# Block sums of a down projection: from GpSimd instructions to accumulating DMAs, and activation differences from GpSimd to VectorE

## The chip, the core and the metric

The kernel runs on one NeuronCore of a Trainium2 chip. Its engines are named as in the profile: PE is TensorE (PEld its weight loads), DVE is VectorE, ACT is ScalarE, POOL is GpSimd, SP is SyncE, which here only issues DMAs. The metric is the device time of one execution in microseconds.

## The reference

One encoder block on 512 tokens of width 1024, in float32. Three token mixers (a bidirectional mLSTM, a neighbourhood attention, a cross-attention into 256 memory tokens) are merged by gates, and a gated feed-forward network with 2816 hidden channels follows:

```python
def conv_glu_ffn(h, w_up, w_conv, b_conv, w_down):
    a, u = jnp.split(h @ w_up, 2, axis=-1)
    return (jax.nn.gelu(dwconv3(a, w_conv, b_conv)) * u) @ w_down
...
x = x + conv_glu_ffn(rms_norm(x, ffn_norm_g[l]), w_ffn_up[l], w_ffn_conv[l], b_ffn_conv[l], w_ffn_down[l])
return rms_norm(x, final_norm_g)
```

The change lies in the last matrix product, `(512 x 2816) @ w_down (2816 x 1024)`, here called the down projection.

## The kernel before

**Three matmuls for one.** A float32 product is made from values split in a high and a low part: `mm3` issues high x high, high x low and low x high (L296, L297, L298). A weight block is loaded raw by SP (L203), its high part is made on ACT (L259 in the down projection, L274 elsewhere), the low part is the difference from the raw block on DVE (L260, L275). The tiles `w` that hold both parts have four buffers, so a block can be split only when PE has finished the block four places earlier.

**The down projection.** Its 2816 rows are 22 slices of 128. The first 12 slices go in six pairs (`NSP = 6`) through seven products of sums and differences instead of eight plain ones, in the manner of Strassen: `FORMS` names, for form 1 to 7, which activation quarters are subtracted, which weight blocks are added (sign 1) or subtracted (sign -1), or that a block is used alone. The last 10 slices (`NOK`) are multiplied plainly. `DOWN` lists 62 weight blocks in the order in which PE takes them; here they are numbered 0 to 61. Form 2 has blocks 0 to 7, form 4 blocks 8 to 16, form 5 blocks 17 to 24, form 7 blocks 25 to 33, form 1 blocks 34 to 42, form 3 blocks 43 to 50, form 6 blocks 51 to 58. In each of them six blocks belong to the form ("s" blocks, 6 matmuls each), and two or three plain ones ("k" blocks, 12 matmuls each) stand between. Blocks 59 to 61 are held for the end.

**Sums.** A block of forms 3, 4, 6 and 7 (24 in all) and of form 1 (6) comes as two blocks of 128x512 side by side in one 512 KB load. `emit_sum` adds or subtracts them into the first one on POOL (L225, `u<-u`, 30 instructions). For forms 1, 2, 5, 6 and 7 it also makes the three activation differences of a form, each for two pairs (L225, `s<-u`, 15 instructions). ACT and DVE split the activations into `uf` (L246, L247), with three pairs of buffers. All 45 sums are made by `in_turn`, which keeps them on POOL in the order of the program, after the last product of the GELU part (L1260).

**Raw tiles.** Blocks 0 to 5 use the three `raw` buffers that the rest of the kernel uses. From block 6 on they lie in "units", 14 big tiles shared with the activations; one unit takes two blocks, wide or narrow. `weights(key)` is called before each block's matmuls; it emits the loads up to 5 blocks ahead (`RAW_AHEAD`, 3, for the earlier ones), the sums up to 3 ahead and the splits up to 2 ahead. A scheduler then sets the order on each engine; every engine and each DMA queue works strictly in that order.

**After a form,** DVE adds its two product tiles into the output tiles `C_` (L1293, where the residual comes in, and L1295). `left` multiplies half of an output row block with the final gain on POOL (L1309, four in all).

Of the kernel before, what the change touches and what calls it, by code (L numbers as in the profile page):

```python
# [14 lines left out]
ALU = mybir.AluOpType  # L15
AX = mybir.AxisListType

P = 128
# [4 lines left out]
M = 256  # L23
DFF = 2816
FT = DFF // P
NSP = 6
NOK = FT - 2 * NSP
HELD = 3
HC = D // 2
# [96 lines left out]
DOWN0 = BINDEX[DOWN[0]][0]  # L126
# [3 lines left out]
def hybrid_block(ctx, tc, xT, memT, wflat, vecs, gbias, nabias, out):  # L130
    nc = tc.nc
    V, A, G, PE, SY = nc.vector, nc.scalar, nc.gpsimd, nc.tensor, nc.sync
# [12 lines left out]
    def nm(s):  # L145
        uid[0] += 1
        return f"{s}_{uid[0]}"

    def unit(dt=F32):
        return up.tile([P, UNIT], dt, tag="unit", name=nm("u"))  # L150

    def scr(n=512):
        return sp.tile([P, 512], F32, tag="scr", name=nm("s"))[:, :n]
# [28 lines left out]

    raws, split = {}, {}
    RAW_AHEAD, SPLIT_AHEAD = 3, 1
    st = {"raw": 0, "sum": DOWN0, "split": 0}
    uraw = []

    def emit_raw(i):
        key, n = BLOCKS[i]
        _, off, _ = BINDEX[key]  # L190
        if i < DOWN0 + NSP:
            r = wp.tile([P, BW], F32, tag="raw", name=nm("wr"), bufs=3)
        else:
            if not uraw:
                u = unit()
                uraw.extend((u[:, :2 * HC], u[:, 2 * HC:4 * HC]))
            r = uraw.pop(0)
        src = wflat[off:off + P * n].rearrange("(p n) -> p n", p=P)
        raws[i] = r
        if i < 2:  # L200
            cuts = (0, P, n // 2, n) if i == 0 else (0, n // 2, n)
            return [(r[:, a:b], src[:, a:b]) for a, b in zip(cuts, cuts[1:])]
        SY.dma_start(r[:, :n], src)  # L203
# [15 lines left out]

    ur, uf = [], {}  # L220

    def in_turn(dst, a, b, op):

        with tc.issue_after(st["g"]):
            st["g"] = G.tensor_tensor(dst, a, b, op=op).ins  # L225

    def emit_sum(i):

        key, n = BLOCKS[i]
        if key[0] != "s":  # L230
            return
        a, a2, _, w2, sign = FORMS[key[1]]
        p = key[2]
        if w2:
            r = raws[i]
            in_turn(r[:, :HC], r[:, :HC], r[:, HC:2 * HC], ALU.add if sign > 0 else ALU.subtract)
        if p % 2 == 0:
            v = ur[p // 2][:, :4 * S].rearrange("p (q k s) -> p q k s", q=2, k=2)
            q2 = lambda t: t.rearrange("p (q s) -> p q s", q=2)
            src = v[:, :, a[1], a[0] * M:(a[0] + 1) * M]  # L240
            if a2:
                d = q2(scr())
                in_turn(d, src, v[:, :, a2[1], a2[0] * M:(a2[0] + 1) * M], ALU.subtract)
                src = d
            h, l = [tp.tile([P, S], F32R, tag="E", name=nm("uf"), bufs=EB) for _ in range(2)]
            A.activation(q2(h), src, AF.Copy)  # L246
            V.tensor_tensor(q2(l), src, q2(h).bitcast(F32), op=ALU.subtract)  # L247
            uf[key[1], p // 2] = h, l
# [31 lines left out]
    def weights(key):  # L280

        i, _, n = BINDEX[key]
        last = len(BLOCKS) - 1
        while st["raw"] <= min(i + (5 if st["raw"] >= DOWN0 + NSP else RAW_AHEAD), last):
            emit_raw(st["raw"])
            st["raw"] += 1
        while st["sum"] <= min(i + 3, last):
            emit_sum(st["sum"])
            st["sum"] += 1
        while st["split"] <= min(i + (2 if st["split"] >= DOWN0 else SPLIT_AHEAD), last):  # L290
            emit_split(st["split"])
            st["split"] += 1
        return split.pop(i)
# [35 lines left out]

    A.dma_start(vec[:, :8], vecs[:, :8])  # L330
    w0, w1 = emit_raw(0), emit_raw(1)
    st["raw"] = 2
    load_x(0)
# [112 lines left out]
    def proj(key, XHs, XLs, n=S, bank=None, at={}):  # L446
        ws = weights(key)
        ps = (bank or mmps)()
        for k in range(KT):
            mm3(ps[:, :n], ws[k][0], ws[k][1], XHs[k], XLs[k], k == 0, k == KT - 1)  # L450
            if k in at:
                at[k]()
        return ps
# [3 lines left out]
    for k in range(KT):  # L457
        if k % 2 == 0:
            ws = weights(("mlq", k // 2))
        while done < min(KT, k + 1 + (k > 2)):  # L460
            x_part(done)
            done += 1
        wh, wl = ws[k % 2]
        for f in range(4):
            fs = slice(f * P, (f + 1) * P)
            mm3(ps_q[f], wh[:, fs], wl[:, fs], XH[k], XL[k], k == 0, k == KT - 1)
# [91 lines left out]
    for c, n in enumerate(TMW):  # L558
        pss = [(mmps if c % 2 else atps)() for _ in range(NT)]
        g = 2 if n == 512 else 4  # L560
# [552 lines left out]
    for f in range(4):  # L1113
# [5 lines left out]
        g = so[0][:, f * S:(f + 1) * S]  # L1119
# [117 lines left out]
    for f in range(FT):  # L1237
# [30 lines left out]
        if 3 <= f < 11:  # L1268
            t, g = (f - 3) % NT, (f - 3) // NT
            turns[t, g] = turn_out(x2v[g][:, :, t * P:(t + 1) * P])  # L1270
        if 6 <= f < 14:
            t, g = (f - 6) % NT, (f - 6) // NT
# [66 lines left out]
    last = NT - 1  # L1339
    for n, key in enumerate(DOWN):  # L1340
        wh, wl = weights(key)
        if key[0] == "s":
            _, i, p = key
            if p == 0 and i < 6:
                pm = [atps() for _ in range(2)]
            dst = pm if i < 6 else px[:2] if i == 7 else px[2:]
# [12 lines left out]
        _, g, j = key  # L1359
# [138 lines left out]
```

## Time and profile before

| | |
|---|---|
| median of 3 runs | 883.09 us (881.12 to 883.58) |
| the profiled execution | 882.28 us, span 880.1 us, mean granted TensorE clock 0.994 |
| down projection, first to last matmul | 735.86 to 871.2 us |
| from the last matmul to the end of the span | 9 us |
| POOL, `u<-u` sums of weight blocks (L225) | 30 instructions, 47.8 us |
| POOL, `s<-u` differences of activations (L225) | 15 instructions, 24.1 us |
| DVE, low parts of the down projection's blocks from units (L260) | 53 instructions, 56.6 us |

A view by stretches gives, for each stretch of the span, its length and how long each engine was busy in it, with the number of instructions in brackets, the granted clock, the DMA engines' busy share and GB/s. Matmuls overlap, so PE's busy time says only where it stood still; the distance from one matmul's start to the next says more. In a timeline a row is: start, duration, engine, line, operation, output and inputs, and in brackets the idle time before it with the instruction that ended it.

### The profile page before, as it was taken

To read this page: it belongs to the slowest core of one execution; us is meant where nothing else is said; L and a number is where in the kernel's file an instruction comes from. 1 tells how busy PE (TensorE), PEld (TensorE's weight loads), DVE (VectorE), ACT (ScalarE), POOL (GpSimd) and SP (SyncE) were. 2 spreads that over 40 slices of the span, in tenths; PEclk is the share of its full clock that TensorE was granted. 3 is DMA by queue.
4 is the path that set the end of the run, shared out by engine and by line. 5 is a ranking of instruction groups with operands and counts; after the bars stand their busy time and mean duration, and the time that the engine had idled before them with its cause. 6 is when DMAs were issued, how large, how long until landed. Compare 5 with 4: busy or idle time off the path is not lost.

```text
span 880.1 us, 12286 instructions
## 1 busy us (share of the span) xinstructions
PE 854.3 (97%) x4044; PEld 712.1 (81%) x4044; DVE 636.9 (72%) x1214; ACT 463.5 (53%) x975; POOL 211.1 (24%) x264
## 2 busy tenths in 40 slices
PE   9999999999999999999999999999999998898985
PEld 7898889988888888888888888888888886676755
DVE  6699677865477768987585477766666667886993
ACT  7465556765455668887444444344444444343442
POOL 1001100000105800760002112111111116465851
PEclk9999999999999999999999999999999999999999
DMA  8237654643346746987434324444322226356532
GB/s 266 91 106 227 205 159 148 199 131 100 128 132 201 189 144 213 253 234 219 150 110 136 107 96 141 147 146 145 117 96 96 96 72 238 96 191 207 212 132 96
DMA packets 73520, 135.75 MB, mean 154 GB/s; under 512 B 9832, under 2 KB 35048, under 8 KB 73456
## 3 DMA queue, kind: packets, MB, share of 16 engines
q1 hardware_dynamic: 65808, 128.51, 45.0%
q0 software_dynamic: 7360, 6.32, 3.4%
q8 instruction: 32, 0.52, 0.3%
q14 instruction: 32, 0.26, 0.1%
q10 hardware_dynamic: 288, 0.14, 0.1%
HBM read 120.23 MB, written 14.70 MB: 153 GB/s over the span
## 4 chain that ended last, share of the span: by engine, by line
PE 84%; DVE 5%; issue 3%; DMA 3%; POOL 2%; ACT 2%; SPq 0%; POOLq 0%; DVEq 0%; ACTq 0%
PE mm L297 25%; PE mm L298 24%; PE mm L296 24%; DVE w L260 2%; DMA u<-wflat 2%; PE at L297 2%; PE at L298 2%; PE at L296 2%; PE at L944 1%; POOL s L225 1%; DVE uf L247 1%; PE at L777 1%; DMA wr<-wflat 1%; PE at L779 1%; PE at L761 1%
## 5 line engine op out<-in xcount | busy, mean ns | idle before, releaser
L296 PE MATMUL mm<-u,w 128*128 128x512 f32 (+1 forms) x912 | 353.8, 388 | 0.4 <-ACT w L274 0.4
L297 PE MATMUL mm<-u,w 128*128 128x512 f32 (+1 forms) x912 | 352.2, 386 | 0.0
L298 PE MATMUL mm<-u,w 128*128 128x512 f32 (+1 forms) x912 | 352.1, 386 | 0.0
L274 ACT ACTIVATE w<-wr 128x512 fp32r<-128x512 f32 (+1 forms) x256 | 159.6, 627 | 146.2 <-PE mm L298 109.1
L275 DVE TENSOR_TENSOR w<-wr,w 128x512 fp32r<-128x512 f32 (+2 forms) x257 | 175.1, 686 | 71.5 <-ACT w L274 69.0
L298 PEld LDWEIGHTS mm<-u,w 128*128 128x128 f32 x912 | 171.4, 188 | 35.0 <-DVE w L275 0.7
L296 PEld LDWEIGHTS mm<-u,w 128*128 128x128 f32 x912 | 171.5, 188 | 34.5 <-ACT w L274 1.1
L297 PEld LDWEIGHTS mm<-u,w 128*128 128x128 f32 x912 | 171.5, 188 | 33.7 <-DVE u L303 0.5
L590 POOL DMA_DIRECT2D u<-nav_d x128 | 62.1, 501 | 102.0 <-PE at L944 51.5
L1260 POOL TENSOR_TENSOR s<-s,rb 128x512 f32<-128x512 f32 x22 | 37.4, 1699 | 188.7 <-DVE s L1259 181.0
L260 DVE TENSOR_TENSOR w<-u,w 128x512 fp32r<-128x512 f32 x53 | 56.6, 1100 | 6.9 <-ACT w L259 6.9
L225 POOL TENSOR_TENSOR u<-u 128x512 f32<-128x512 f32 x30 | 47.8, 1612 | 31.6 <-DVE w L260 20.3
L259 ACT ACTIVATE w<-u 128x512 fp32r<-128x512 f32 x53 | 32.4, 624 | 35.5 <-PE mm L298 23.2
L297 PE MATMUL mm<-w,u 128*128 128x512 f32 x116 | 46.0, 397 | 4.6 <-DVE w L260 4.5
L296 PE MATMUL mm<-w,u 128*128 128x512 f32 x116 | 45.6, 394 | 0.0
L298 PE MATMUL mm<-w,u 128*128 128x512 f32 x116 | 45.2, 390 | 0.0
L297 PEld LDWEIGHTS mm<-w,u 128*128 128x128 f32 x116 | 21.9, 189 | 11.5 <-DVE w L260 7.2
L1228 POOL TENSOR_TENSOR acc<-acc,s 128x512 f32<-128x512 f32 x7 | 9.0, 1288 | 91.6 <-ACT s L1227 91.6
L483 ACT ACTIVATE s<-pad,vec 128x512 f32<-128x512 f32 x30 | 24.4, 813 | 6.2 <-DVE pad L481 5.3
L246 ACT ACTIVATE uf<-s 128x512 fp32r<-128x512 f32 x15 | 9.4, 629 | 32.4 <-POOL s L225 31.3
L296 PE MATMUL at<-w,uf 128*128 128x512 f32 x60 | 24.2, 403 | 2.3 <-ACT uf L246 2.3
L296 PEld LDWEIGHTS mm<-w,u 128*128 128x128 f32 x116 | 21.9, 189 | 4.7
(300 smaller groups left out, 1238.0 us busy)
## 6 DMA issues: line engine op xcount, KB each, us to landing
wr<-wflat SPq DMA_DIRECT2D x124, 512.0 KB, 3.4
u<-wflat SPq DMA_DIRECT2D x30, 512.0 KB, 4.4
td<-s SPq DMA_DIRECT2D x160, 64.0 KB, 2.0
U<-td SPq DMA_DIRECT2D x40, 256.0 KB, 3.6
u<-wflat SPq DMA_DIRECT2D x26, 256.0 KB, 3.3
s<-xT SPq DMA_DIRECT2D x24, 256.0 KB, 4.2
nab<-nabias SPq DMA_DIRECT2D x16, 256.0 KB, 4.0
u<-nav_d POOLq DMA_DIRECT2D x128, 32.0 KB, 3.7
```

Of the source, the lines that this page charges most:

```text
L225: st["g"] = G.tensor_tensor(dst, a, b, op=op).ins
L246: A.activation(q2(h), src, AF.Copy)
L259: A.activation(h, r[:, :HC], AF.Copy)
L260: V.tensor_tensor(l, r[:, :HC], h.bitcast(F32), op=ALU.subtract)
L274: A.activation(h[:, u:v], src, AF.Copy)
L275: V.tensor_tensor(l[:, u:v], src, h[:, u:v].bitcast(F32), op=ALU.subtract)
L296: PE.matmul(ps, lh, rh, start=start, stop=False)
L297: PE.matmul(ps, lh, rl, start=False, stop=False)
L298: st["mm"] = PE.matmul(ps, ll, rh, start=False, stop=stop).ins
L483: A.activation(t1, pad[:, 0:512], AF.Identity, scale=vcol(w, i), bias=vcol(b, i))
L590: G.dma_start(vw[r * 32:(r + 1) * 32, i * 256:(i + 1) * 256], nav_v[hf, r, CW[b]:CW[b] + 32, hp * 256:(hp + 1) * 256])
L1260: st["g"] = G.tensor_tensor(c, c, rb2, op=ALU.mult).ins
```

## The change

The 24 sums of weight blocks with sign 1 are no longer made by an instruction. SP loads only the first block (256 KB) of the two; the second one is fetched from HBM by a DMA of POOL's queue that adds into the first block's tile (`accum_op`, L236 of the changed kernel). It can be issued only when the first block has landed. The 6 subtractions of form 1 and the 15 differences of activations become DVE instructions (L247 and L254 there). A unit now takes four blocks (two for form 1), loads run up to 9 blocks ahead, the accumulating DMAs are emitted up to 5 ahead, and subtractions and differences up to 3 ahead. `in_turn` is gone; POOL keeps the accumulating DMAs in order among themselves and after the last L1260 (now L1274).

```diff
-    st = {"raw": 0, "sum": DOWN0, "split": 0}
+    st = {"raw": 0, "sum": DOWN0, "form": DOWN0, "split": 0}
...
+        src = wflat[off:off + P * n].rearrange("(p n) -> p n", p=P)
         if i < DOWN0 + NSP:
             r = wp.tile([P, BW], F32, tag="raw", name=nm("wr"), bufs=3)
         else:
+            both = key[:2] == ("s", 1)
+            if both and len(uraw) % 2:
+                uraw.pop(0)
             if not uraw:
                 u = unit()
-                uraw.extend((u[:, :2 * HC], u[:, 2 * HC:4 * HC]))
-            r = uraw.pop(0)
-        src = wflat[off:off + P * n].rearrange("(p n) -> p n", p=P)
+                uraw.extend((u, j * HC) for j in range(4))
+            u, a = uraw.pop(0)
+            if both:
+                uraw.pop(0)
+            r = raws[i] = u[:, a:a + HC * (2 if both else 1)]
+            if n > HC and not both:
+                st[i] = src
+                src = src[:, :HC]
+                n = HC
...
-    def in_turn(dst, a, b, op):
-
-        with tc.issue_after(st["g"]):
-            st["g"] = G.tensor_tensor(dst, a, b, op=op).ins
-
     def emit_sum(i):
+
+        if i in st:
+            with tc.issue_after(st["g"]):
+                st["g"] = G.dma_start(raws[i], st.pop(i)[:, HC:], accum_op=ALU.add).ins
+
+    def emit_form(i):
...
-        if w2:
+        if sign < 0:
             r = raws[i]
-            in_turn(r[:, :HC], r[:, :HC], r[:, HC:2 * HC], ALU.add if sign > 0 else ALU.subtract)
+            V.tensor_tensor(r[:, :HC], r[:, :HC], r[:, HC:2 * HC], op=ALU.subtract)
...
             if a2:
                 d = q2(scr())
-                in_turn(d, src, v[:, :, a2[1], a2[0] * M:(a2[0] + 1) * M], ALU.subtract)
+                V.tensor_tensor(d, src, v[:, :, a2[1], a2[0] * M:(a2[0] + 1) * M], op=ALU.subtract)
                 src = d
...
-        while st["raw"] <= min(i + (5 if st["raw"] >= DOWN0 + NSP else RAW_AHEAD), last):
+        while st["raw"] <= min(i + (9 if st["raw"] >= DOWN0 + NSP else RAW_AHEAD), last):
             emit_raw(st["raw"])
             st["raw"] += 1
-        while st["sum"] <= min(i + 3, last):
+        while st["sum"] <= min(i + 5, st["raw"] - 1):
             emit_sum(st["sum"])
             st["sum"] += 1
+        while st["form"] <= min(i + 3, last):
+            emit_form(st["form"])
+            st["form"] += 1
```

PE's order is unchanged, and so is every engine's up to about the last step of the feed-forward's up projection. Three places show how the rest moves.

POOL's queue from the last GELU product on, before (`s_...<-u_...` is a difference of activations, `u_...<-u_...` a sum of weight blocks):

```order
L1260 TENSOR_TENSOR s_7196<-s_7196,rb_5543 128x512
L225 TENSOR_TENSOR s_7208<-u_5382 128x512
L225 TENSOR_TENSOR s_7266<-u_5383 128x512
L225 TENSOR_TENSOR u_7295<-u_7295 128x512 x2
L225 TENSOR_TENSOR u_7316<-u_7316 128x512
L225 TENSOR_TENSOR u_7357<-u_7357 128x512
L225 TENSOR_TENSOR u_7391<-u_7391 128x512 x2
L225 TENSOR_TENSOR s_7464<-u_5381 128x512
```

The same place in the changed kernel (L1274 is the GELU product, L1323 the product with the final gain):

```order
L1274 TENSOR_TENSOR s_7196<-s_7196,rb_5543 128x512
L236 DMA u_7283<-wflat 128x512 x2
L236 DMA u_7288<-wflat 128x512 x2
L236 DMA u_7322<-wflat 128x512 x2
L236 DMA u_7448<-wflat 128x512
L236 DMA u_7517<-wflat 128x512 x3
L236 DMA u_7573<-wflat 128x512 x2
L236 DMA u_7751<-wflat 128x512
L1323 TENSOR_TENSOR u_7246<-u_7246,gf_7247 128x512
```

Where POOL computed 45 sums it now issues 24 DMAs; the first two are for blocks 8 and 9, which lie in `u_7283`.

DVE where form 2 ends and form 4 begins, before (L260 low part of a block, L247 of activations, L1293 the additions after form 2; `w_7344`, `w_7359` and `w_7380` are blocks 8, 9 and 10):

```order
L260 TENSOR_TENSOR w_7323<-u_7283,w_7323 128x512
L260 TENSOR_TENSOR w_7344<-u_7295,w_7344 128x512
L260 TENSOR_TENSOR w_7359<-u_7295,w_7359 128x512
L1293 TENSOR_TENSOR u_7246<-U_6173,at_7256 128x512
L1293 TENSOR_TENSOR u_7246<-U_6260,at_7257 128x512
L1293 TENSOR_TENSOR u_7246<-U_6509,at_7256 128x512
L1293 TENSOR_TENSOR u_7246<-U_6591,at_7257 128x512
L260 TENSOR_TENSOR w_7380<-u_7316,w_7380 128x512
```

And in the changed kernel (L271 low part of a block, L258 of activations, L254 a difference of activations, L1307 the additions; `w_7349` and `w_7364` are blocks 8 and 9):

```order
L271 TENSOR_TENSOR w_7328<-u_7283,w_7328 128x512
L258 TENSOR_TENSOR uf_7381<-u_5382,uf_7380 128x512
L271 TENSOR_TENSOR w_7349<-u_7283,w_7349 128x512
L254 TENSOR_TENSOR s_7466<-u_5381 128x512
L254 TENSOR_TENSOR s_7496<-u_5382 128x512
L254 TENSOR_TENSOR s_7541<-u_5383 128x512
L254 TENSOR_TENSOR s_7586<-u_5381 128x512
L1307 TENSOR_TENSOR u_7246<-U_6173,at_7256 128x512
L1307 TENSOR_TENSOR u_7246<-U_6260,at_7257 128x512
L1307 TENSOR_TENSOR u_7246<-U_6509,at_7256 128x512
L1307 TENSOR_TENSOR u_7246<-U_6591,at_7257 128x512
L271 TENSOR_TENSOR w_7364<-u_7283,w_7364 128x512
```

Block 9's low part, which stood ahead of the four additions, now stands behind them, and four differences for the later forms 5 and 1 stand there too; block 8's waits for the first accumulating DMA.

DVE a little earlier, in the last GELU step, in the changed kernel (L1271 and L1273 belong to the GELU, L1280 takes POOL's product, `w_7272` and `w_7291` are blocks 3 and 4):

```order
L1271 SCALAR_TENSOR_TENSOR s_7200<-s_7200,s_7196 128x512
L258 TENSOR_TENSOR uf_7211<-s_7208,uf_7210 128x512
L254 TENSOR_TENSOR s_7266<-u_5383 128x512
L1273 SCALAR_TENSOR_TENSOR s_7196<-s_7200,s_7196 128x512
L271 TENSOR_TENSOR w_7272<-wr_7251,w_7272 128x512
L258 TENSOR_TENSOR uf_7269<-s_7266,uf_7268 128x512
L1280 TENSOR_TENSOR s_7196<-mm_7217,s_7196 128x512
L271 TENSOR_TENSOR w_7291<-wr_7264,w_7291 128x512
```

The differences of form 2 (`s_7208`, two rows above the first one shown, and `s_7266`) and a low part of activations have come in ahead of L1273, which POOL's last GELU product waits for.

## The prediction

> **What bounds the kernel now.** First the page: the engines' shares and the slices.
>
> ```profile
> PE 854.3 (97%) x4044; PEld 712.1 (81%) x4044; DVE 636.9 (72%) x1214; ACT 463.5 (53%) x975; POOL 211.1 (24%) x264
> PE   9999999999999999999999999999999998898985
> POOL 1001100000105800760002112111111116465851
> ```
>
> PE is the bound everywhere but in the last seven slices, where POOL becomes busy. Those slices are the down projection, so I cut it into stretches at PE's longer gaps. Columns: length, then busy us (and instructions) of PE, PEld, DVE, ACT, POOL, granted clock, DMA share, GB/s.
>
> ```profile
> 735.85:871.20 135.35, 120.03 (x502) 93.56 (x500) 106.61 (x120) 53.00 (x96) 79.33 (x51) 0.97 0.47 161
> ...
> 735.85:749.40 13.55, 10.59 (x38) 7.92 (x37) 11.53 (x11) 7.03 (x12) 11.92 (x8) 0.87 0.57 211
> 749.40:761.00 11.60, 9.02 (x38) 6.50 (x36) 11.60 (x11) 3.98 (x7) 7.92 (x5) 1.00 0.31 90
> 761.00:789.30 28.30, 28.30 (x125) 23.40 (x126) 21.52 (x29) 11.05 (x19) 11.40 (x8) 1.00 0.57 186
> 789.30:806.00 16.70, 13.30 (x53) 9.45 (x52) 10.39 (x12) 5.24 (x10) 9.52 (x7) 0.96 0.40 132
> 806.00:820.00 14.00, 14.00 (x58) 11.31 (x57) 11.26 (x16) 8.10 (x16) 11.12 (x7) 0.92 0.67 238
> 820.00:834.00 14.00, 11.88 (x51) 9.14 (x50) 14.00 (x17) 4.91 (x10) 11.61 (x9) 1.00 0.73 263
> 834.00:851.00 17.00, 12.74 (x50) 8.93 (x51) 16.70 (x14) 7.85 (x14) 14.72 (x9) 1.00 0.49 170
> 851.00:871.20 20.20, 20.20 (x98) 16.92 (x96) 9.62 (x18) 4.85 (x10) 1.12 (x2) 1.00 0.07 27
> ```
>
> What would these matmuls take without a gap? PE's timeline gives the pace: the first two rows are 11 starts apart, 2.49 us, so 0.2264 us each; after a gap (third row) come starts 0.42 us apart (the last two).
>
> ```profile
> 735.86 0.39 PE L296 MATMUL at<-w,uf 128*128 128x512 f32 x1
> ...
> 738.35 0.39 PE L298 MATMUL at<-w,uf 128*128 128x512 f32 x1
> 741.08 0.50 PE L296 MATMUL at<-w,uf 128*128 128x512 f32 x1 [2.34 <-ACT uf L246]
> ...
> 743.97 0.63 PE L297 MATMUL at<-w,uf 128*128 128x512 f32 x1
> 744.39 0.63 PE L298 MATMUL at<-w,uf 128*128 128x512 f32 x1
> ```
>
> The stretch runs 502 matmuls, one of them mostly before it, and 18 (6 on each of three lines, at the end) are half as wide: 483 x 0.2264 + 18 x 0.113 = 111.4 us, and the last one's own end 0.3, against 135.35. PE loses **23.6 us**. By stretch (length less count x 0.2264): 4.9, 3.0, 0, 4.7, 0.9, 2.5, 5.7, and 0 at the end; the rest is matmuls that a border counts twice. The long loss-free stretch 761 to 789 matters most. It contains the same kinds of blocks.
>
> Who ends these gaps, among PE's waits from 735.8 to 871.2 (total, times, longest):
>
> ```profile
> PE mm L297 <- DVE w L260: 10.5, 8, 3.0
> PE at L296 <- ACT uf L246: 2.3, 1, 2.3
> ```
>
> So the low part of a block comes late from DVE. DVE is busy for 97 of the 115 us up to 851: not the bound in sum, but in places. Its timeline and POOL's say why:
>
> ```profile
> 745.92 1.77 DVE L260 TENSOR_TENSOR w<-wr,w 128x512 fp32r<-128x512 f32 x1
> 752.72 5.15 DVE L260 TENSOR_TENSOR w<-u,w 128x512 fp32r<-128x512 f32 x3
> 757.80 2.46 DVE L1293 TENSOR_TENSOR u<-U,at 128x512 f32<-128x512 f32 x4
> 761.39 1.88 DVE L260 TENSOR_TENSOR w<-u,w 128x512 fp32r<-128x512 f32 x3
> ...
> 742.03 10.22 POOL L225 TENSOR_TENSOR u<-u 128x512 f32<-128x512 f32 x6
> 752.21 5.11 POOL L225 TENSOR_TENSOR s<-u 128x512 f32<-128x512 f32 x3
> 774.95 1.74 POOL L225 TENSOR_TENSOR u<-u 128x512 f32<-128x512 f32 x1 [17.63 <-DVE w L260]
> ```
>
> While POOL computes (742 to 757.3, at 1.70 us an instruction), DVE's low parts also go one per 1.7 us; when POOL stops, the same instruction takes 0.63 (three in 1.88). The two engines take turns. From 757.3 to 774.95 POOL rests, and there PE loses nothing after 761. This is the present bound of the stage: 45 sums on POOL, which are slow themselves and slow DVE.
>
> **The change part by part.** *Removed:* 45 POOL instructions, 47.8 + 24.1 us, and with them DVE's slow turns.
>
> ```profile
> L260 DVE TENSOR_TENSOR w<-u,w 128x512 fp32r<-128x512 f32 x53 | 56.6, 1100 | 6.9 <-ACT w L259 6.9
> L225 POOL TENSOR_TENSOR u<-u 128x512 f32<-128x512 f32 x30 | 47.8, 1612 | 31.6 <-DVE w L260 20.3 <-DMA u<-wflat 11.1
> L225 POOL TENSOR_TENSOR s<-u 128x512 f32<-128x512 f32 x15 | 24.1, 1615 | 0.0
> ```
>
> *Added on DVE:* 6 + 15 instructions of the same shape, at the undisturbed spacing of 0.61 to 0.63 us (757.80 and 761.39 above): 13 us. DVE then has about 104 instructions up to 851 (110 in the stretches above, less those counted twice) plus 20 of the new ones, 124 x 0.61 = 76 us, in the 91.5 us that PE needs for that part (115.15 - 23.6). That is 83%. In 761 to 789 DVE was 76% busy, partly against POOL, and PE lost nothing, so I expect few losses; the in-order places must be looked at singly.
>
> *Block 4.* DVE's L1280 waits for POOL's last GELU product, and block 4's low part stands behind it. Before:
>
> ```profile
> 731.50 0.69 DVE L481 TENSOR_TENSOR pad<-mm,rb 128x512 f32<-128x512 f32 x1
> 736.71 0.69 DVE L1259 SCALAR_TENSOR_TENSOR s<-s,s 128x512 f32<-128x512 f32 x1 [0.70 <-ACT s L1258]
> 737.48 1.66 POOL L1260 TENSOR_TENSOR s<-s,rb 128x512 f32<-128x512 f32 x1 [8.48 <-DVE s L1259]
> ```
>
> Three more DVE instructions now stand ahead of L1259 (L1273 of the changed kernel), 1.8 us, of which 0.7 fits into the wait shown: POOL's product ends at about 739.14 + 1.1 = 740.2, block 4's low part is there two DVE steps later, 741.5. PE reaches block 4 after four blocks of 6 x 0.227 = 1.36 us, at 741.3, and needs the low part 0.23 later: 0 to 0.7 us lost, I take 0.3. In return the 2.34 us wait of 741.08 goes: the differences of form 2 no longer queue behind that product.
>
> *Blocks 8 and 9.* The first two accumulating DMAs are issued at 740.2, one after the other. No accumulating DMA is in the trace. The nearest are POOL's plain 128x512 DMAs, first row their time on POOL, second from issue to landing, and SP's loads of two blocks and of one:
>
> ```profile
> L540 POOL DMA_DIRECT2D nav_d<-nv x8: 531/532/782, 85.6 to 98.1; - x8
> DMA to landing us min/median/max: 2.5/3.7/4.7
> ...
> u<-wflat SPq DMA_DIRECT2D x30, 512.0 KB, 4.4
> u<-wflat SPq DMA_DIRECT2D x26, 256.0 KB, 3.3
> ```
>
> Reading the destination as well makes it 512 KB of reads: bounds 2.5 us (nothing extra) and 4.7 + 4.4 = 9.1 us (a second pass after the first), I take 4.7, nearest the POOL rows. Block 8 lands at 745, its parts are made by 746.3 (ACT 0.63, DVE 0.69); PE wants it at 735.86 + 13.6 = 749.5. Then DVE does four differences and four additions, 8 x 0.61 = 4.9, and block 9's low part is ready at about 751.8; PE wants it at 749.5 + 1.36 + 0.23 = 751.1. Lost: 0.7, up to 5 with a 9.1 us landing; I take 1.2.
>
> *Later blocks.* A unit holds four blocks (two in form 1) and at least four units take turns, so the load of a first half can go out eight blocks or more (over 14 us) before its use: 3.3 for the load and even 9.1 for the accumulation are hidden. POOL's queue holds only these 24 DMAs (24 x 0.53 = 13 us) and four products of L1309. After each form, four additions (2.5 us) stand ahead of a low part that PE wants 4 to 5.4 us after the form's last product: covered. I allow 2.0 for what I have not seen (0 to 4.5).
>
> *DMA engines.* The share times length over the stretches up to 851 is 62 us of full use. A plain 256 KB takes 0.76 us of all 16 engines (161 GB/s at share 0.47). Taking 24 away leaves 44. POOL's own queue is slower per byte, 6.32 MB in 3.4% of the span, 1.24 us for 256 KB:
>
> ```profile
> q0 software_dynamic: 7360, 6.32, 3.4%
> ```
>
> So one accumulation costs between 0.76 and 2 x 1.24 = 2.5 us of all engines; I take 1.5 (one read more at the plain rate): 44 + 36 = 80 us of 95, hidden.
>
> *Half clock.* In 735.85 to 749.4 and 806 to 820 the granted clock is below 1; the timeline has 18 starts that lie 0.35 to 0.5 apart like those of 743.97, together 3.4 us of the 23.6. Gaps of 2 us should be gone: 0.5 left (0 to 3.4).
>
> Sum: 0.3 + 1.2 + 2.0 + 0.5 = 4.0 us left of 23.6, so **19.6 us gained**. 882.28 (the profiled execution; 0.8 under the median of 883.09) - 19.6 = 862.7, as a median 863.5. Everything ahead of 735 and the 9 us behind the last matmul stay.
>
> **The rivals.** *Late accumulations (R1).* The landing is 9 us instead of 4.7, blocks 8 and 9 cost 4 us more, and DVE, waiting in order at block 8, shifts what follows: 868 to 872. For it: an operation that no row shows. Against: the later ones are still early.
>
> *DMA engines decide (R2).* With price c per accumulation the stage needs 44 + 24c; beyond 95.5 us (c = 2.15) the engines set the end. At my upper bound of 2.5 that is 104, a time of 872; at c = 3.0 the gain is gone. *Slower (R3)* is the same resource beyond that point: at c = 3.4, some 4.5 times a plain copy, 125.6 us against 115.15, 893. For it: only the silence of the trace; against: 2.5 already counts every byte twice at the slow queue's rate.
>
> *The gaps stay (R4).* They come from in-order queues and splits only two blocks ahead, not from POOL, and the 13 us on DVE fill what POOL left: 874 to 883. For it: DVE at 83%. Against: 761 to 789.
>
> *POOL starves (R5).* If descriptors had to wait for DVE, each issue would wait for an instruction of 0.69 or for several. But while DVE did the same low parts (19 of them at 678 ns), POOL issued its 128 DMAs evenly:
>
> ```profile
> L275 DVE TENSOR_TENSOR w<-wr,w 128x512 fp32r<-128x512 f32 x19 | 12.8, 678 | 1.0 <-ACT w L274 0.9
> ...
> L590 POOL DMA_DIRECT2D u<-nav_d x128: 489/493/583, 273.8 to 398.7; - x128
> ```
>
> Three instructions' wait for each of the first two would cost 2 x 2.1 = 4.2 us at block 9: 868. The Trainium skill speaks against this change here: "SBUF — State Buffer", section "Summary: rules for kernel authors", tells authors who hide a GpSimd-issued DMA under a DVE operation to use the other queues, since descriptor generation starves while DVE is in a 2x or 4x mode. By that rule R5 would be likely; the trace does not agree for this instruction, 583 ns being the longest of the 128.
>
> **How the numbers follow.** Forecast 0.58 (860 to 868); R1 0.10; R2 0.11; R4 0.08; R5 0.03; R3 0.10. Time 863.5. The low end is every loss gone (23.6 off, 859.5), rounded to 860; the high end takes in R1, R5, R2 to past c = 2.5 and some of R4, 877; R3, the end of R2 and half of R4 are left out, 0.19. About 0.3% (2.6 us) is what a measurement can tell from no change. Faster: forecast, R1, R5, R2 but 0.01 and 0.04 of R4, 0.85; same 0.05; slower R3, 0.10.
>
> **What would show it.** Right: no L225-like work on POOL, 24 DMAs there of about half a us each; low parts (L271) at 0.6 to 0.7 us throughout; PE's loss from 735.9 to the last matmul 2 to 6 us, most of it before 753. Wrong: PE or ACT waiting for accumulated blocks beyond block 12 (R2, R3, with the DMA share near 1), DVE without a gap while PE waits (R4), POOL DMAs of over 1 us (R5). If accumulations take over 2.15 us of all engines each, the forecast falls.

## The result and the profile after

The changed kernel takes 871.26 us (median of 4 runs, 869.96 to 872.84) beside 883.34 us for the kernel before (881.12 to 884.72). The ratio is 0.9866, with a 95% interval from 0.984 to 0.9893. The change makes the kernel faster by 12.1 us, where 19.6 were predicted; the time lies inside the predicted range, 7.8 us above the predicted time.

The profiled execution took 871.15 us, its span is 869.4. The page of the changed kernel, the engines' shares and POOL's slices:

```profile
PE 851.0 (98%) x4044; PEld 713.2 (82%) x4044; DVE 619.4 (71%) x1235; ACT 464.1 (53%) x975; POOL 160.1 (18%) x243
...
POOL 2001100000104810742001202111111111221401
```

POOL's last seven slices, which read 6465851 before, now read 1221401. The down projection in stretches of the changed kernel (columns as before: length, then busy us and instructions of PE, PEld, DVE, ACT, POOL, granted clock, DMA share, GB/s; the last row is the whole of it):

```profile
735.07:748.60 13.53, 13.53 (x61) 11.22 (x60) 9.54 (x17) 6.89 (x13) 7.62 (x7) 1.00 1.07 326
748.60:761.00 12.40, 10.02 (x38) 7.77 (x37) 11.24 (x19) 4.70 (x8) 1.11 (x2) 0.86 0.83 191
761.00:789.30 28.30, 28.30 (x127) 23.43 (x126) 20.44 (x33) 13.25 (x22) 4.12 (x5) 1.00 0.71 188
...
802.00:819.00 17.00, 14.28 (x56) 11.30 (x55) 12.73 (x16) 6.98 (x13) 9.00 (x10) 0.90 0.92 233
819.00:834.00 15.00, 12.50 (x51) 9.15 (x51) 8.02 (x16) 6.71 (x15) 5.13 (x5) 1.00 1.01 227
...
735.07:840.00 104.93, 96.57 (x404) 77.38 (x403) 77.93 (x123) 47.15 (x84) 28.40 (x29) 0.97 0.78 205
735.07:860.50 125.43, 117.07 (x502) 94.58 (x500) 86.85 (x138) 52.60 (x95) 29.52 (x31) 0.97 0.67 176
```

In PE's timeline the first and the last start of a matmul lie 125.2 us apart. Less the 111.4 us that the matmuls need, PE loses **13.8 us**, where it lost 23.7 before: of the 12.1 us, 9.9 come from this stage in the two profiled executions. The stage also starts 0.8 us earlier (735.07 instead of 735.86); over all kernels below its start varies from 735.07 to 736.88, so a difference of a microsecond between two of them can arise ahead of it. The loss sits in three places, 748 to 761, 802 to 819 and 819 to 836; the stretches between lose nothing. Who ends PE's gaps (total, times, longest):

```profile
PE mm L311 <- DVE w L271: 3.5, 2, 2.7
PE at L311 <- DVE w L271: 2.9, 3, 2.4
PE at L310 <- ACT w L270: 2.0, 2, 1.7
```

**First place: block 9.** Here are POOL's and DVE's rows of the changed kernel, one fence each:

```profile
736.65 2.28 POOL L1274 TENSOR_TENSOR s<-s,rb 128x512 f32<-128x512 f32 x1 [9.61 <-DVE s L1273]
738.87 5.39 POOL L236 DMA_DIRECT2D u<-wflat  x6
```

```profile
746.66 0.69 DVE L271 TENSOR_TENSOR w<-u,w 128x512 fp32r<-128x512 f32 x1 [2.80 <-ACT w L270]
747.27 2.49 DVE L254 TENSOR_TENSOR s<-u 128x512 f32<-128x512 f32 x4
749.68 2.48 DVE L1307 TENSOR_TENSOR u<-U,at 128x512 f32<-128x512 f32 x4
752.07 1.89 DVE L271 TENSOR_TENSOR w<-u,w 128x512 fp32r<-128x512 f32 x3
```

POOL's last GELU product ends at 738.9, and six accumulating DMAs are issued behind it. The first one, issued at 738.87 for block 8, lands after 7.0 us, the second one, for block 9, after 8.3; the DMA engines' share is 1.07 in that stretch. DVE stands still for 2.80 us, until block 8 has landed and ACT has made its high part, takes block 8 at 746.66, then the eight instructions that stand ahead of block 9, whose low part is started at 752.07. PE stands still for 2.5 us, and for some microseconds behind it the granted clock is low (0.86 in that stretch).

**Second place: DVE beside POOL's products.** DVE and POOL around 801:

```profile
800.81 5.53 DVE L271 TENSOR_TENSOR w<-u,w 128x512 fp32r<-128x512 f32 x1
```

```profile
801.13 1.62 POOL L1323 TENSOR_TENSOR u<-u,gf 128x512 f32<-128x512 f32 x1
802.38 2.12 POOL L236 DMA_DIRECT2D u<-wflat  x2
803.52 2.26 POOL L1323 TENSOR_TENSOR u<-u,gf 128x512 f32<-128x512 f32 x1
```

One low part lasts 5.53 us instead of 0.69. It ends when the second of two products with the final gain does; between the products POOL issues two accumulating DMAs. PE stands still for 2.9 us.

**Third place: a held block.** ACT's instructions for blocks 59 and 60, which PE needs only at the end, and a row of the chain (the waits, followed back from the last instruction):

```profile
827.65 0.63 ACT L270 ACTIVATE u<-u 128x512 fp32r<-128x512 f32 x1 [6.59 <-DMA u<-wflat]
829.55 0.63 ACT L270 ACTIVATE u<-u 128x512 fp32r<-128x512 f32 x1 [0.75 <-DMA u<-wflat]
```

```profile
817.17 12.35 DMA u<-wflat
```

ACT waits 6.59 us for the plain load of block 59, which was issued at 816.67 and took 10.9 us while the DMA engines were full (share 1.01 from 819 to 834). The chain's row is the load of block 60, 12.35 us; block 61's took 13.9. Blocks 47 to 50 are queued behind the parts of these held blocks, on ACT or on DVE, and PE waits for blocks 47, 48 and 50 in five gaps of 1.87, 0.50, 0.42, 0.58 and 0.92 us, 4.3 us together.

What the new operations cost, from the groups, queues and DMA issues of the page, and from the view of L236 (duration in ns least/median/most; landing in us in the last row):

```profile
L271 DVE TENSOR_TENSOR w<-u,w 128x512 fp32r<-128x512 f32 x53 | 40.5, 779 | 23.5 <-ACT w L270 23.3
...
q0 software_dynamic: 10816, 12.61, 7.7%
...
u<-wflat SPq DMA_DIRECT2D x50, 256.0 KB, 5.4
u<-wflat POOLq DMA_DIRECT2D x24, 256.0 KB, 8.4
```

```profile
L236 POOL DMA_DIRECT2D u<-wflat x24: 853/902/2563, 738.9 to 824.1; - x24
...
DMA to landing us min/median/max: 4.1/8.4/13.2
```

The low parts went from 1100 to 779 ns. An accumulation takes POOL 0.9 us and lands after 8.4 us; the queue's share gives (7.7% x 869.4 - 3.4% x 880.1) / 24 = 1.54 us of all 16 DMA engines for each.

### The profile page after: what moved, and what is told of

It is laid out like the page before. It is cut to its first block, busy times and chain, and to the rows that moved or that the text cites. A ratio compares the mean times of both kernels' runs of the same rounds, so it can differ in the third digit from the quotient of the medians.

```text
span 869.4 us, 12253 instructions
## 1 busy us (share of the span) xinstructions
PE 851.0 (98%) x4044; PEld 713.2 (82%) x4044; DVE 619.4 (71%) x1235; ACT 464.1 (53%) x975; POOL 160.1 (18%) x243
## 3 DMA queue, kind: packets, MB, share of 16 engines
q0 software_dynamic: 10816, 12.61, 7.7%
## 4 chain that ended last, share of the span: by engine, by line
PE 89%; DMA 3%; issue 3%; DVE 3%; ACT 1%; POOL 1%; SPq 0%; POOLq 0%; DVEq 0%; ACTq 0%
PE mm L311 25%; PE mm L310 25%; PE mm L312 25%; DMA u<-wflat 3%; PE at L311 3%; PE at L312 2%; PE at L310 2%; DVE w L271 1%; PE at L958 1%; PE at L791 1%; PE at L793 1%; PE at L775 1%; POOL s L1274 0%; PE at L925 0%; PE at L924 0%
## 5 line engine op out<-in xcount | busy, mean ns | idle before, releaser
L1274 POOL TENSOR_TENSOR s<-s,rb 128x512 f32<-128x512 f32 x22 | 37.9, 1721 | 190.0 <-DVE s L1273 182.3
L271 DVE TENSOR_TENSOR w<-u,w 128x512 fp32r<-128x512 f32 x53 | 40.5, 779 | 23.5 <-ACT w L270 23.3
L236 POOL DMA_DIRECT2D u<-wflat x24 | 21.4, 1175 | 62.4 <-DVE u L1309 27.3
L311 PEld LDWEIGHTS mm<-w,u 128*128 128x128 f32 x116 | 22.2, 192 | 8.9 <-DVE w L271 4.3
L312 PEld LDWEIGHTS mm<-w,u 128*128 128x128 f32 x116 | 22.2, 191 | 4.7
L310 PEld LDWEIGHTS mm<-w,u 128*128 128x128 f32 x116 | 22.2, 192 | 4.6
```

The source lines that it names most:

```text
L236: st["g"] = G.dma_start(raws[i], st.pop(i)[:, HC:], accum_op=ALU.add).ins
L271: V.tensor_tensor(l, r[:, :HC], h.bitcast(F32), op=ALU.subtract)
L310: PE.matmul(ps, lh, rh, start=start, stop=False)
L311: PE.matmul(ps, lh, rl, start=False, stop=False)
L312: st["mm"] = PE.matmul(ps, ll, rh, start=False, stop=stop).ins
L1274: st["g"] = G.tensor_tensor(c, c, rb2, op=ALU.mult).ins
```

## The experiments

PE's loss is worked out as above for each kernel: the distance from the first to the last start in the down projection less 111.4 us.

| kernel | median us (lowest to highest) | ratio to before (95%) | PE's loss |
|---|---|---|---|
| changed kernel | 871.26 (869.96 to 872.84) | 0.9866 (0.984 to 0.9893) | 13.8 |
| 1 differences alone on DVE | 873.55 (872.01 to 874.24) | 0.9891 (0.9872 to 0.991) | 15.2 |
| 2 accumulating DMAs alone | 880.65 (879.43 to 881.54) | 0.9971 (0.9961 to 0.998) | 22.5 |
| 3 all sums on DVE | 860.78 (860.13 to 861.94) | 0.9752 (0.9731 to 0.9773) | 2.5 |
| 4 plain DMAs | 862.56 (861.8 to 864.03) | 0.9771 (0.9754 to 0.9787) | 4.8 |
| 5 no second blocks | 858.71 (858.15 to 859.12) | 0.9723 (0.9709 to 0.9738) | 0.1 |
| 6 final gain on DVE | 871.8 (871.36 to 873.73) | 0.9876 (0.9861 to 0.9891) | 13.9 |
| 7 held blocks' parts late | 863.12 (861.65 to 865.08) | 0.9775 (0.9754 to 0.9795) | 6.1 |
| 8 as 7, accumulations early | 862.52 (861.61 to 863.6) | 0.9756 (0.9736 to 0.9776) | 3.8 |
| 9 as 8, final gain on DVE | 861.25 (860.56 to 862.45) | 0.9744 (0.9727 to 0.9761) | 3.2 |
| 10 as 3, final gain on DVE | 858.42 (858.29 to 858.72) | 0.9711 (0.9697 to 0.9726) | 0.3 |
| 11 as 9, only two of them early | 860.39 (859.8 to 861.34) | 0.9742 (0.9726 to 0.9759) | 1.4 |

The kernel before beside them had medians from 883.02 to 883.96.

### 1 and 2: the two parts of the change, each alone

Experiment 1 is the kernel before with the differences moved:

```diff
-                in_turn(d, src, v[:, :, a2[1], a2[0] * M:(a2[0] + 1) * M], ALU.subtract)
+                V.tensor_tensor(d, src, v[:, :, a2[1], a2[0] * M:(a2[0] + 1) * M], op=ALU.subtract)
```

> The kernel before with one part of the change: the 15 differences of activations on VectorE, the 30 sums of weight blocks still on GpSimd. If GpSimd's computing instructions cost the time (themselves and by slowing VectorE), a third of them is gone (24 of 72 us) and the wait of 2.3 us near block 2 too: PE's loss in the down projection falls from 23.6 to about 16, 875 us (871 to 879). If only the accumulating DMAs bring the gain, nothing changes: 882 to 884.

Experiment 2 is the changed kernel with the differences back on POOL:

```diff
-                V.tensor_tensor(d, src, v[:, :, a2[1], a2[0] * M:(a2[0] + 1) * M], op=ALU.subtract)
+                with tc.issue_after(st["g"]):
+                    st["g"] = G.tensor_tensor(d, src, v[:, :, a2[1], a2[0] * M:(a2[0] + 1) * M], op=ALU.subtract).ins
```

> The changed kernel with the 15 differences of activations left on GpSimd, in one order with the accumulating DMAs. By the same theory 24 us of GpSimd computing come back, each of these instructions slows one or two of VectorE to 1.7 us and stands ahead of DMAs: loss about 17 to 20 us instead of 13.8, 875 us (872 to 879). If the differences are indifferent: 871.

Measured: 873.55 and 880.65. PE's waits in experiment 1, all for low parts (the 2.34 us wait for ACT is gone):

```profile
PE at L297 <- DVE w L260: 8.2, 6, 3.4
PE mm L297 <- DVE w L260: 2.4, 2, 1.7
```

The 15 differences alone bring 9.8 us, the accumulating DMAs alone 2.7, outside what was expected (some 8, at least 4); together 12.5, about the 12.1 of the whole change. In experiment 2 the first rows are PE's longest waits, then one row of DVE and two of POOL:

```profile
PE at L311 <- ACT w L271: 7.9, 1, 7.9
PE at L311 <- ACT uf L258: 2.3, 1, 2.3
```

```profile
743.77 6.80 DVE L272 TENSOR_TENSOR w<-wr,w 128x512 fp32r<-128x512 f32 x1
```

```profile
742.04 5.44 POOL L236 DMA_DIRECT2D u<-wflat  x6
745.50 6.20 POOL L255 TENSOR_TENSOR s<-u 128x512 f32<-128x512 f32 x3
```

The third place is here too, as one gap of 7.9 us (the chain of waits passes through a load of 12.93 us). What holds DVE at the second place is here at 744, a DVE instruction of 6.80 us that lasts through most of POOL's accumulating DMAs and of the three differences behind them. So the smaller gain lies with the accumulating DMAs, not with the differences.

### 3: every sum on DVE

```diff
-        with tc.issue_after(st["g"]):
-            st["g"] = G.tensor_tensor(dst, a, b, op=op).ins
+        V.tensor_tensor(dst, a, b, op=op)
```

It is the kernel before, with this edit in `in_turn` alone: all 45 sums become DVE instructions, and the 512 KB loads stay.

> The kernel before with all 45 sums on VectorE and no accumulating DMA, units and load order as before. VectorE then has about 78 + 24 x 0.61 = 93 us of work in the first 105 us of the stage, but the accumulations (8.4 us to landing) and their load on the DMA engines are gone. Theory A, the accumulating DMAs only replace one slow place by another: as fast as the change, 868 to 873. Theory B, VectorE is then too full in order: loss over 17 us, 875 to 881.

Measured: 860.78, faster than both theories allowed. The stretch of the down projection up to 840:

```profile
735.00:840.00 105.00, 103.55 (x454) 84.79 (x453) 95.44 (x154) 50.42 (x89) 7.93 (x5) 1.00 0.59 204
```

DVE is busy for 95.4 of 105 us and PE loses 2.5 in all. A DVE at 91% does not hold PE up here, and this kernel with 24 DVE additions (24 x 0.61 = 14.6 us of DVE) is 10.5 us faster than the changed one with 24 accumulating DMAs. The two also differ in the sizes of the loads and in how far they run ahead, so the 10.5 us are the price of the whole arrangement. Beside experiment 1, the 30 block sums on DVE instead of POOL bring 12.8 us.

### 4 and 5: what of the accumulation costs time

Experiment 4 lets the same DMAs overwrite instead of add, so it leaves out the first block of each of these 24 sums; experiment 5 leaves out the DMAs, and with them the second blocks.

```diff
-                st["g"] = G.dma_start(raws[i], st.pop(i)[:, HC:], accum_op=ALU.add).ins
+                st["g"] = G.dma_start(raws[i], st.pop(i)[:, HC:]).ins
```

> The changed kernel with the 24 DMAs of GpSimd's queue as plain copies instead of accumulating ones (the second block overwrites the first, so the sums of the weight blocks are left out): same bytes, queue, order and waits. If adding is what makes them slow, landing falls from 8.4 us to 4 or 5, the DMA engines' time per DMA from 1.55 us to 0.8, and the loss of 2.5 us at block 9 and of about 4 us in the last forms shrink: 865 us (862 to 868). If the shared DMA engines' bursts are the cause and not the adding, landing stays over 7 us and the time at 870 to 872.

```diff
-            with tc.issue_after(st["g"]):
-                st["g"] = G.dma_start(raws[i], st.pop(i)[:, HC:], accum_op=ALU.add).ins
+            st.pop(i)
```

> The changed kernel without the 24 DMAs (second blocks are neither loaded nor added; their part of the sum is left out). The bound for all costs of the accumulation: the gap at block 9 and those in the last forms go if they come from it, the 2.9 us gap at 803 us stays if it comes from the two products with the final gain on GpSimd: loss 13.8 to about 5, 862 us (860 to 866). If the late held blocks are the fault of the order on ScalarE alone, about 4 us stay: 866 to 868.

Measured: 862.56, inside the first theory's interval, and 858.71, below what was expected. Experiment 4's queue and issue rows of the page, and its view of L236 (POOL time):

```profile
q0 software_dynamic: 9280, 12.61, 5.5%
...
u<-wflat SPq DMA_DIRECT2D x50, 256.0 KB, 4.5
u<-wflat POOLq DMA_DIRECT2D x24, 256.0 KB, 6.1
```

```profile
L236 POOL DMA_DIRECT2D u<-wflat x24: 536/536/652, 739.0 to 817.6; - x24
```

The plain DMA takes POOL 0.54 us instead of 0.90, (5.5% x 860.6 - 29.9) / 24 = 0.73 us of all DMA engines instead of 1.54, and 6.1 us to landing instead of 8.4 (4 or 5 were expected). So 8.7 of the 12.5 us between the changed kernel and experiment 5 come from the adding, 3.9 from the second blocks' transfers. With the same product on POOL ahead of and behind two DMAs, no low part takes longer than 1.88 us in experiment 4. In experiment 5 the products with the final gain stay on POOL, and the gap at 803 us, which was expected to stay with them, is gone: without DMAs beside them they hold no low part longer than 1.78 us. Block 9 is not late there either, with the same order on DVE. 858.7 is about the floor for this order of PE's work: PE loses 0.1.

### 6: the products with the final gain on DVE

```diff
-        G.tensor_tensor(cv(t, 0), cv(t, 0), gfin[0], op=ALU.mult)
+        V.tensor_tensor(cv(t, 0), cv(t, 0), gfin[0], op=ALU.mult)
```

> The changed kernel with the four products with the final gain (L1323) on VectorE. In the trace VectorE's low part of a block started at 800.8 us takes 5.5 us while GpSimd runs product, two DMAs, product. If GpSimd's reads block it, the 2.9 us gap there and the half clock behind it (about 1.3 us) go: 867.5 us (866 to 869). If it is something else that stops VectorE there (the DMAs' descriptors), the gap stays: 871.

Measured: 871.8, no gain, the time of the second theory, but the gap is gone. The view of the low parts, and PE's waits:

```profile
L271 DVE TENSOR_TENSOR w<-u,w x53: 681/686/694, 742.3 to 847.2; 128x512 fp32r<-128x512 f32 x53
```

```profile
PE at L310 <- ACT w L270: 3.5, 1, 3.5
PE at L311 <- DVE w L271: 3.1, 1, 3.1
PE mm L311 <- DVE w L271: 1.6, 2, 1.0
```

No low part is longer than 0.69 us, so the accumulating DMAs hold nothing without POOL's products, as the products held little without the adding (experiments 4 and 5): the 5.53 us took both. The gap at 803 is gone, but the wait for ACT at the held block, 2.0 us in two gaps before, is now one of 3.5, and block 9's has grown to 3.1. PE reached the third place 2.1 us earlier, and the load of block 59 landed at 827.2, hardly earlier than the 827.5 of the changed kernel. A cause can be shown right while its removal gains nothing.

### 7: the held blocks' parts behind block 58's

```diff
-            A.activation(h, r[:, :HC], AF.Copy)
-            V.tensor_tensor(l, r[:, :HC], h.bitcast(F32), op=ALU.subtract)
+            if key[0] == "k" and key[1] == 1 and key[2] >= NOK - HELD:
+                with tc.issue_after(st["a"]):
+                    st["a"] = A.activation(h, r[:, :HC], AF.Copy).ins
+                with tc.issue_after(st["v"]):
+                    st["v"] = V.tensor_tensor(l, r[:, :HC], h.bitcast(F32), op=ALU.subtract).ins
+            else:
+                st["a"] = A.activation(h, r[:, :HC], AF.Copy).ins
+                st["v"] = V.tensor_tensor(l, r[:, :HC], h.bitcast(F32), op=ALU.subtract).ins
```

> The changed kernel with the high and low parts of the three held blocks made after those of block 58 on ScalarE and VectorE (they stood ahead of blocks 47, 48 and 49, and the first waited 6.6 us for its load). If ScalarE's order there is the cause, the gaps of 827 to 836 us (4.3 us) go: 867 us (865.5 to 868.5). If the accumulations of blocks 47 to 49 are late by themselves, the gaps stay: 870 to 871.5.

Measured: 863.12, faster than both theories allowed. PE's waits, the stretch of the third place and the view of the low parts:

```profile
PE at L317 <- DVE w L277: 3.3, 2, 2.6
```

```profile
819.00:834.00 15.00, 15.00 (x66) 12.14 (x66) 13.39 (x20) 7.26 (x12) 5.16 (x5) 1.00 1.00 229
```

```profile
L277 DVE TENSOR_TENSOR w<-u,w x53: 675/684/3447, 742.3 to 839.4; 128x512 fp32r<-128x512 f32 x53
```

No wait for ACT is left. The DMA engines are as full as before (share 1.00 from 819 to 834), and PE is busy throughout: nothing that it needs is queued behind the held blocks' loads now. The gain of 8.1 us is more than the 4.3 of the five gaps. In this profile the gap beside POOL's products costs 0.9 instead of 2.9, and the starts at half clock (0.35 to 0.5 us apart) cost 1.6 instead of 3.0. DVE's rows there:

```profile
802.28 2.43 DVE L277 TENSOR_TENSOR w<-u,w 128x512 fp32r<-128x512 f32 x1
804.64 3.13 DVE L254 TENSOR_TENSOR s<-u 128x512 f32<-128x512 f32 x1
```

The same product, two accumulating DMAs and product hold DVE for as long as before, but here one low part got through between the two products. Why it did was not tried.

### 8, 9 and 11: the accumulating DMAs ahead of the last GELU product

Experiment 8 takes experiment 7 and ties the accumulating DMAs only to one another:

```diff
-            with tc.issue_after(st["g"]):
-                st["g"] = G.dma_start(raws[i], st.pop(i)[:, HC:], accum_op=ALU.add).ins
+            with ExitStack() as chain:
+                if "acc" in st:
+                    chain.enter_context(tc.issue_after(st["acc"]))
+                st["acc"] = G.dma_start(raws[i], st.pop(i)[:, HC:], accum_op=ALU.add).ins
```

> The kernel with held blocks' parts moved back (863.12 us, PE's loss 6.08: 2.75 at block 9, 0.86 beside POOL's product, half clock 2.0), and in addition the accumulating DMAs no longer tied behind POOL's last GELU product, only to one another, so the first four are issued ahead of it. Theory A (block 9 is late because its accumulating DMA is issued at 739 and six of them then share the way, about 7 us to landing): issued earlier, blocks 8 and 9 are there in time, the gap of 2.75 and the half clock after it go: 859 (858.4 to 860). Theory B (block 9 is late because DVE has four differences and four additions ahead of its low part, whenever the block lands): DVE's order stays, the gap stays at 1.5 to 2.75: 861.5 to 863.5.

Measured: 862.52, as the second theory had it, but not for its reason. The gap of 2.75 at block 9 is gone; in its place stands one of 1.85 at block 4, since POOL's last GELU product now waits behind four DMAs. Because PE reaches block 9 later by that much, this run alone does not say how much of the old gap was the landing.

Experiment 9 moves the product with the final gain to DVE as well (the edit of experiment 6).

> The changed kernel with all three causes found taken away together: held blocks' parts after block 58's, accumulating DMAs free of the last GELU product, and the product with the final gain on VectorE instead of POOL. Theory A (these three are the whole loss of 13.8 us): PE's loss under 1 us, 858.5 (858 to 859.5), the floor that the kernel without second blocks had. Theory B (24 accumulations with 1.55 us of all engines each, at a DMA share near 1 between 805 and 834, still cost something of their own): a loss of 2 to 5 us moves to a block of forms 1, 3 or 6 that lands late: 861 to 864, no better than 860.78 with VectorE additions.

Measured: 861.25, in the second theory's interval. PE's only wait is the one at block 4, and POOL's rows show why:

```profile
PE at L319 <- DVE w L279: 2.7, 1, 2.7
```

```profile
740.25 0.87 POOL L238 DMA_DIRECT2D u<-wflat  x1 [1.19 <-DMA u<-wflat]
740.81 1.60 POOL L1282 TENSOR_TENSOR s<-s,rb 128x512 f32<-128x512 f32 x1
```

The product that started at 736.65 in the changed kernel starts at 740.81, after a DMA that waited for its first block to land. The loss is neither gone (first theory) nor in a late block of forms 1, 3 or 6 (second theory).

Experiment 11 lets only two of the DMAs go ahead of that product:

```diff
+            st["n"] = st.get("n", 0) + 1
             with ExitStack() as chain:
+                if st["n"] > 2:
+                    chain.enter_context(tc.issue_after(st["g"]))
                 if "acc" in st:
```

> The previous kernel without the three causes (861.25 us) lost 3.19, of it 2.83 at block 4: VectorE waited 4.46 us for POOL's last GELU product, which stood behind four accumulating DMAs, each waiting for its first block's load (issued at 734.35, 738.20, 740.25 and 740.8 there). Here only two of them are issued ahead of that product. Theory A (the rest of the loss is this place in POOL's queue): the product starts after the second, at about 739.1 instead of 740.8, 1.7 us earlier; of 2.83 some 1.1 stay at block 4, blocks 8 and 9 still land before DVE gets to them; loss 1.2 to 1.8, 859.5 (859 to 860.3). Theory B (accumulations cost something that moves elsewhere when a gap is closed, as the held block's load did before): the loss stays at 3, 861 or more.

Measured: 860.39 and a loss of 1.4; the loss is what the first theory had, the time 0.1 above its interval. One wait is left, at block 9; it and an earlier row of ACT:

```profile
PE at L322 <- DVE w L282: 0.5, 1, 0.5
```

```profile
742.62 0.63 ACT L281 ACTIVATE w<-wr 128x512 fp32r<-128x512 f32 x1 [2.59 <-DMA wr<-wflat]
```

DVE does not stand still for block 8 here, and block 9 still comes 0.5 late behind the eight instructions. DVE came to them late: ACT and DVE had waited for the plain load of block 5, which took 6.7 us. In experiment 5, where DVE has the same order and no second block shares the engines, block 9 is in time. So the 2.5 us at block 9 came from the landing, not from DVE's order. In this kernel the 24 accumulations stay as slow as before (7.9 us to landing in the median), and PE loses 1.4 us in all: an accumulating DMA costs time where the order of a queue makes something else wait for it.

### 10: no POOL products and no accumulating DMAs

It is experiment 3 with the product with the final gain on DVE (the edit of experiment 6).

> The kernel before with all 45 sums on VectorE (860.78 us, PE's loss 2.46, VectorE busy 95 of 105 us), and in addition the product with the final gain on VectorE, so POOL computes nothing in the down projection after the GELU part. Theory A (the two remaining gaps of 0.76 and 0.99 come from VectorE being 91% busy): four more instructions cost 4 x 0.6 = 2.4 us of VectorE, no gain, 860.5 to 862.5. Theory B (they come from turns with POOL's products): gaps gone, 858.7 to 859.7.

Measured: 858.42, as the second theory had it and 0.3 below its interval, the fastest kernel of all, 25.5 us under the kernel before beside it. The stretch up to 840 and the view of the sums of weight blocks:

```profile
735.00:840.00 105.00, 105.00 (x464) 86.69 (x463) 95.20 (x159) 50.78 (x89) 1.70 (x1) 1.00 0.58 205
```

```profile
L224 DVE TENSOR_TENSOR u<-u x30: 679/684/693, 732.7 to 829.5; 128x512 f32<-128x512 f32 x30
```

With four more instructions DVE's busy time is the same as in experiment 3 (95.2 against 95.4), since only one instruction is longer than 0.8 us where experiment 3 had five, and PE has no gap above 0.2. It computes what the kernel before computes. Experiment 11, the best one with accumulating DMAs, is some 2 us behind, of which 1.1 are PE's loss; the two intervals touch at 0.9726.

## Why the prediction was right or wrong

**Right: the bound, and where the gain comes from.** The stage was bound by sums on POOL that take turns with DVE. With all of them and the other POOL products gone, PE loses 0.3 of its 23.7 us (experiment 10). Matmuls need 111.4 us; the floor of 859.5 that the prediction gave, every loss gone, was met by experiments 5 and 10 (858.7 and 858.4). But the two parts of the change are unequal: the 15 differences, a third of POOL's work, bring 9.8 us, the 24 accumulating DMAs 2.7 (experiments 1 and 2). Of the prediction's own signs of being right, the DMAs of half a us, the low parts at 0.6 to 0.7 us throughout and a loss of 2 to 6 us, most of it before 753, did not come. That the time fell inside the range is owed to its width, which took in the rivals' times.

**Right: DVE's room (against R4).** Predicted were 124 instructions and 76 us of DVE in 91.5; there were 123 and 77.93 us in 104.93. Even 159 instructions at 91% cost PE nothing in experiment 10.

**Right: the DMA engines in sum, wrong by place (against R2 and R3).** 1.5 us of all engines for an accumulation was taken, 1.54 measured; 80 us of use were predicted, 0.78 x 104.93 = 82 measured. But the sum was put against the whole stage and called hidden. The loads come in bursts of four blocks, with accumulations between them: the share is 1.07 from 735 to 748.6 and 1.01 from 819 to 834, and there plain loads take 9.2 to 13.9 us. Hidden in the mean, it is not hidden at the third place.

**Block 4: 0.3 predicted, nothing lost.** POOL's product ended at 738.9 instead of 740.2, and the wait of 2.34 us went as predicted.

**Block 9: 1.2 predicted, 2.5 lost.** The step that failed is the landing of 4.7 us: block 8's accumulation took 7.0. The 4.7 came from POOL's rows at 85 to 98 us; at block 8 the DMA engines' share is 1.07, and the plain DMA at the same place took 6.0 (experiment 4), so 1.3 of the 2.3 us are there without the adding and 1.0 comes with it. That six are issued together is not the cause for block 8, the first of them: one by one, in experiment 8, the first six took 6.7 to 7.6. Block 9's parts came 1.0 us later than worked out (752.8 instead of 751.8) and PE came 0.8 earlier (750.3 instead of 751.1); with the 0.7 of the working that makes 2.5. The bounds of 2.5 to 9.1 held the median of 8.4 but not the longest, 13.2.

**The allowance of 2.0 for what was not seen: 8.3 lost.** This is the term that was wrong. It holds the second place (2.9), the third (4.3) and about 1.1 in gaps under 0.3. Both places lie in the order of the queues. Four products stay on POOL among the accumulations, and the turns of DVE with POOL's products were the prediction's own main finding; the prediction counted these products and gave them no price. And "hidden" was said of the loads by their lead over their own use, without asking what is queued behind an instruction that waits for one: block 59's part stands ahead of blocks 47 to 50, which PE needs first.

**Half clock: 0.5 predicted, 3.0 lost** (15 starts that lie 0.35 to 0.5 us apart). It was to go with the gaps of 2 us, and these were not gone: half clock followed the gaps at block 9 (2.5) and beside POOL's products (2.9). But the prediction's link is loose: no half clock followed the wait of 2.7 us in experiment 9, nor that of 3.04 us at 850 in the kernel before. The sum: 0 + 2.5 + 8.3 + 3.0 = 13.8 instead of 4.0.

**R1, late accumulations,** had the right time (868 to 872) by chance: it wanted 9 us to landing and 4 us more at blocks 8 and 9, where 7.0 and 8.3 us to landing cost 1.3 more than forecast; experiment 7, which leaves the accumulations where they are, gains 8.1 us. **R5:** POOL's DMAs took 0.9 us, not half a us as predicted and not over 1 us in the median either (the longest was 2.56). What was seen to wait is DVE, for POOL. The rule that the prediction set beside R5 is tied to a 2x or 4x mode of DVE; the prediction did not show these subtractions to be in one, so it did not make R5 likely. **R3** had no run near it.

## What to carry to other kernels

When work leaves an engine, look for what stays on that engine: two of the four products left on POOL, with accumulating DMAs between them, held DVE long enough to cost PE 2.9 us. Price each wait of an in-order queue by what stands behind the waiting instruction, and a DMA's load by the stretch in which it falls, not by its share of the stage. And compare the plainest alternative: 24 additions on an engine with room for them cost next to nothing here (experiments 3 and 10), while their DMA form cost 10 us more as first written, and still some 2 after three places in the queues had been put right (experiment 11).

## What was not expected of the hardware

**An accumulating DMA** of 256 KB (HBM into a float32 tile) took POOL 0.90 us to issue, 1.54 us of all 16 DMA engines and 8.4 us to landing; the plain one at the same places took 0.54, 0.73 and 6.1. The packets of the queue were (10816 - 7360) / 24 = 144 for each, against 80 for the plain one.

**A DVE instruction held across POOL's DMAs.** In the changed kernel a DVE instruction of 0.69 us lasted 5.53 us, over a product on POOL, two accumulating DMAs and a second product; in experiment 2 one lasted 6.80 us. In experiment 7 two instructions shared the same stretch (2.43 and 3.13 us). With plain DMAs between the same products the longest was 1.88. The Trainium skill, "SBUF — State Buffer", section "Who interferes with whom", has a DVE instruction with two SBUF inputs blocked by a GpSimd instruction that reads SBUF, until that one finishes. Experiments 4 and 6 agree with it (1.88 us beside one product, 0.69 without any). That the wait lasted past one product and its DMAs is more than the page says. Why it did with the adding alone, and why not every time, stays open.

**Loads under a full share.** Plain 256 KB loads of SP's queue, 3.3 us in the median before, took 9.2 to 13.9 us where accumulations and a burst of loads shared the engines (four loads issued from 816.3 to 817.7).
